# Seven block products in place of eight for the second half's in-projection of a hybrid decoder trunk

## The chip, the cores and the metric

The kernel runs on one core of a Trainium2 chip. The metric is the device time of one execution in microseconds (us), lower is better. PE is the matrix engine, DVE the vector engine, ACT the scalar engine, POOL and SP the engines that in this kernel mostly issue DMAs.

## The reference

One layer of a decoder trunk over 2048 positions of 1024 channels (D_MODEL), one batch. A first projection gives 3584 channels: 1024 each for the recurrent unit's input and its gate, 512 each for the short convolution's b, c and x.

```python
h = rms_norm(x, norm1_g)
z = h @ w_in                                   # 1024 -> 3584
lru_x, lru_gate, sc_b, sc_c, sc_x = split(z)
lru_x = causal_dwconv(lru_x, lru_conv_w) + lru_conv_b      # 4 taps
r = sigmoid(lru_x @ wa + ba); i = sigmoid(lru_x @ wx + bx) # 64x64 per head
a = exp(-8 r softplus(-lam)); h_t = a_t h_{t-1} + sqrt(1 - a_t^2) i_t lru_x_t
y_mix = [h * gelu(lru_gate), sc_b * causal_dwconv(sc_c * sc_x, sc_conv_w)]
x = x + y_mix @ w_out                          # 1536 -> 1024
u = causal_dwconv(rms_norm(x, norm2_g) @ w_up, ffn_conv_w) # 1024 -> 6144, 3 taps
gate, up = split(u)
x = x + (gelu(gate) * up) @ w_down             # 3072 -> 1024
return rms_norm(x, final_g)
```

## The kernel before

Channels lie on the partitions and positions on the free axis; x comes transposed. The positions are done in two halves of 1024 (T), and a half in two blocks of 512 (NB). Every product of two float32 numbers is made of three matmuls of rounded parts: `split(hi, lo, src)` copies the operand to its rounded high part on ACT and subtracts that from it on DVE for the low part; then hi x hi, hi x lo and lo x hi are summed in PSUM.

The program's stages in order: the in-projection and mixers of half 0 (`in_phase(0, ...)`), the out-projection of half 0 (`sweeps(0, ..., "o", ...)`, "output sweep 0"), the same two for half 1, then for each half an up phase (`up_phase`) and a down sweep.

`in_phase` walks over 12 units (`UNITS`): 8 units L (a 128-channel piece of the recurrent unit: input, convolution, gates, scan) and 4 units S (short convolution). For each product it loads a 512 KB column of w_in (`load_weights`, `load_parts`), splits it and runs 8 contraction steps x 3 matmuls x 2 blocks of 128x512 = 48 matmuls (`product_step`, L238). 28 products make a half. `lru_gates` (L320) runs the gate matmuls of 64 rows, `lru_scan` the sigmoids, exp, root and the scan. The results y of pairs of units are combined (`combine_even`, `combine_odd`) into sums for the out-projection and stored to DRAM (`y_d`); such stores wait in a list (`defer`) and are issued a few steps later by `tick`.

Out-projection, up and down already work by blocks: a 2x2 block product takes seven products of sums for eight. The sums of the weights, S1 to S4, are made by accumulating DMAs (`sum_step`, w_out's during half 0, w_down's during half 1, a piece is loaded to DRAM through SP, and the addition is issued on POOL) or, in the up phase, by DVE (`up_weights`). The up phase's products are `Pair`s: the terms W11, S1, S2, S3, W22, S4, W12 of 12 matmuls each (L613), whose running sums are copied from PSUM by ACT (L624) and added by DVE (L628). `h_prep` makes the right operands for it: x2 times gain and 1/rms, the differences and sums of its blocks, split. In output sweep 0 x of half 1 is prepared (`x_prep`) and its squares are summed; the sweeps also sum the squares of x2 (`add_squares`).

A sweep goes through seven groups of three steps; each step loads 512 KB of weights and 512 KB of y (`wrw_o`, `wrf_o`), splits both (`wh_o`, `wl_o`, `fh_o`, `fl_o`) and runs 24 matmuls (L733).

The order on PE, SP and POOL is as the program is written; that on ACT and DVE is set by a scheduler with priorities (`high_priority`, the constants HP, HW and so on). Buffers are pages of 128x1024 in tagged pools: "act" 28, "w" 10 for split weights, "tmp" 7, and raw tiles `wr`, 4 of three blocks each. A tile waits until the page that it takes is free.

Of the kernel before, what the change touches and what calls it, by code (L numbers as in the profile page):

```python
# [12 lines left out]
P = 128  # L13
# [9 lines left out]
UNITS = [(u[0], int(u[1])) for u in "L0 L1 S0 L2 L3 S1 L4 L5 L6 L7 S2 S3".split()]  # L23
EPS = 1e-6
HP = 120
HALVES = (slice(0, P // 2), slice(P // 2, P))
# [27 lines left out]
PLACE = {"11": (0, 0), "12": (0, 1), "21": (1, 0), "22": (1, 1)}  # L54

# [14 lines left out]
def block_kernel(  # L70
# [43 lines left out]
    sd_d = blocks("sd_d", S_OPS, NI)  # L114
    x2_d = [[dr.tile([2, P, T], F32, name=f"x2_d{h}_{m}") for m in range(KC // 2)] for h in range(NH)]
# [10 lines left out]

    def wpage(name):
        return page(name, "w", 10)
# [7 lines left out]
    def raw_tile(name):  # L136
        return sb.tile([P, 3, NB], F32, name=name, tag="wr", bufs=4)
# [7 lines left out]
    def flat(t):  # L145
        return t.rearrange("p a b -> p (a b)")
# [34 lines left out]
    waiting = []  # L181
    pieces = []
# [3 lines left out]
    def defer(n, dst, src):  # L186
        waiting.append([n, dst, src])

    def tick():
        for w in waiting:  # L190
            w[0] -= 1
        due = [w for w in waiting if w[0] <= 0]
        waiting[:] = [w for w in waiting if w[0] > 0]
        for _, dst, src in due:
            nc.sync.dma_start(dst, src)
# [9 lines left out]

    gate_w = []

    def load_gates():
        gate_w.append(flat(tmp("gw")).rearrange("p (c k) -> p c k", c=NLRU))
        nc.sync.dma_start(gate_w[0], w_gate.rearrange("c p k -> p c k"))  # L210
# [14 lines left out]
    def load_weights(src, name):  # L225
        out = next(load_parts(src, name, 1))
        tick()
        return out

# [73 lines left out]
    def lru_conv(c, half, ps, rs):  # L303
# [3 lines left out]
        cv = flat(act(f"cv{half}_{c}"))  # L307
# [8 lines left out]
    def lru_gates(c, half, cv):  # L316
        pss = [pst2(f"z{name}{half}_{c}") for name in "ri"]
        for t in range(T // NB):
            for ps, rows in zip(pss, HALVES):
                nc.tensor.matmul(ps[t], gate_w[0][rows, c, :], cv[rows, blk(t)], start=True, stop=True)  # L320
        return pss

    def lru_scan(c, half, cv, g, *gates):
        n = f"{half}_{c}"
        r, i, a = (flat(act(f"{x}{n}")) for x in "ria")
# [20 lines left out]
        nc.scalar.activation(g, g, AF.Gelu_apprx_tanh)  # L346
        nc.vector.tensor_tensor(h, g, h, ALU.mult)
        return h
# [9 lines left out]
    def in_product(o, half, acts):  # L358
        ps = pst2(f"zin{half}_{o}")
        wts = load_weights(w_in[o], f"in{half}_{o}")  # L360
# [10 lines left out]
    def sc_first(s, half, acts, rs, ps):  # L371
# [3 lines left out]
        pr = with_halo(f"pr{half}_{s}", 2, half, p_halo[:, s, :], 1, nc.vector)  # L375
# [36 lines left out]
    def in_phase(half, acts, acc, between):  # L412
        if half == 0:
            acts = []
            raws = [raw_tile(f"wr_{half}_{i}") for i in range(3)]
            firsts = (0, NLRU, 1)
            loads = [
                load_parts(w_in[o], f"in{half}_{o}", KC // 2, tile_=t) for o, t in zip(firsts, raws)
            ]
            wts = [None, None, None]  # L420
            pss = [pst2(f"zin{half}_{o}") for o in firsts]
            xs = []
            for k in range(KC):
                def first_part():
                    wts[0] = next(loads[0])

                hi, lo, x = x_prep(half, k, 2 if k < 2 else 1, None if k else first_part)
                acts.append((hi, lo))
                xs.append(x)
                for i in range(1, 3) if k == 0 else range(2 if k in (1, 3, 5) else 0):  # L430
                    wts[i] = next(loads[i])
                for ps, wt in zip(pss[: 3 if k < 2 else 2], wts):
                    product_step(ps, wcol(wt, k), acts[k], k == 0, k == KC - 1)
                if k == 2:
                    nc.sync.dma_start(prm, par[:, KC:])
            for k in range(KC):
                x_square(half, k, acc, xs[k])
            for _ in loads[2]:
                pass
            load_gates()  # L440
        else:
            pss = [in_product(o, half, acts) for o in (0, NLRU)]
        parts = mean_split(acc, f"a{half}")
        rss = []

        def mean():
            rss.append(inv_rms(acc, f"a{half}", parts))
            nc.gpsimd.tensor_copy(mark, rss[0][:, 0:1])
            ready.append(True)

        if half == 0:
            mean()
            ps_2 = pss[2]
            for k in range(2, KC):
                product_step(ps_2, wcol(wts[2], k), acts[k], False, k == KC - 1)
            sum_step()
        else:
            ps_2 = None
            mean()
        rs = rss[0]  # L460
        cv = lru_conv(0, half, pss[0], rs)
        if half == 0:
            decay_rates(dz)
        cur = (cv, lru_gate(0, half, pss[1], rs))
        ps_n = None
        for n, (kind, c) in enumerate(UNITS):
            nxt = UNITS[n + 1] if n + 1 < len(UNITS) else None
            if kind == "L":
# [6 lines left out]
                gates = lru_gates(c, half, cv)  # L475
# [5 lines left out]
            else:  # L481
                pr = sc_first(c, half, acts, rs, ps_n)
                y = sc_second(c, half, acts, rs, pr)
# [4 lines left out]
            last = n >= NOUT - 2  # L488
            if n % 2 == 0:
                even, yc = y, flat(tmp(f"yc{half}_{n}"))  # L490
                combine_even(y_d[half], 4 if last else 7, n // 2, even, yc)
            else:
# [546 lines left out]
```

## Time and profile before

| | |
|---|---|
| median of 3 runs | 2273.15 us (2273.06 to 2275.95) |
| profiled execution | 2274.76 us |
| its span | 2273.0 us |
| granted clock of PE | 0.998 |
| busy time of PE, DVE, ACT, POOL | 2256.1, 1703.8, 1161.1, 138.0 us |
| in-projection of half 0 and output sweep 0 | 0 to 330, 330 to 444 us |
| in-projection of half 1 and output sweep 1 | 444 to 767, 767 to 884 us |
| up, down of half 0 | 884 to 1341, 1341 to 1570 us |
| up, down of half 1 | 1570 to 2029, 2029 to 2273 us |

The span runs from the first to the last instruction in the trace of one execution; the execution's own time is a little longer. A row of groups gives an engine's line and operation, the tile written and those read, shapes, a count, and after the bar the busy time, the mean of one in ns, and the idle time before them with what ended it. A row of the chain gives start, duration and the number of instructions run through.

### The profile page before, as it was taken

The numbers are of one execution on the slowest core, as the hardware profiler recorded it, in microseconds if no ns is written. First come the engines' busy times: TensorE is split into PE (matmuls) and PEld (weight loads), VectorE is DVE, ScalarE is ACT, GpSimd is POOL, SyncE is SP. The second block draws the span as 40 slices with busy tenths as digits, with TensorE's granted clock in tenths as the row PEclk, the third lists the DMA queues.
The fourth block names the chain that finished last, engine by engine and source line by source line (L and its number), as shares of the span: only waits on it lengthen the run. The fifth ranks groups of instructions, "written<-read, shape, count | busy, mean of one in ns | idle before, by whom it ended". The sixth has DMA issues, their size and how long they took to land.

```text
span 2273.0 us, 26022 instructions
## 1 busy us (share of the span) xinstructions
PE 2256.1 (99%) x9918; PEld 1847.4 (81%) x9918; DVE 1703.8 (75%) x1924; ACT 1161.1 (51%) x1279; POOL 138.0 (6%) x188
## 2 busy tenths in 40 slices
PE   9999999999999999999999999999999999999997
PEld 7877788878877888888888888888888888888886
DVE  8765668757657798888888887586888888876556
ACT  7564825565576355544444444354544444443343
POOL 0100000011000000111111100000100000000000
PEclk9999999999999999999999999999999999999999
DMA  8732238768754585233333357675233232359755
GB/s 280 189 95 76 105 129 297 273 163 216 208 116 148 177 284 201 97 110 100 105 104 102 107 197 257 212 252 193 70 102 116 89 118 91 116 183 322 259 195 176
DMA packets 145180, 376.69 MB, mean 166 GB/s; under 512 B 13920, under 2 KB 16608, under 8 KB 144480
## 3 DMA queue, kind: packets, MB, share of 16 engines
q1 hardware_dynamic: 135120, 356.17, 45.2%
q0 software_dynamic: 9792, 18.88, 5.2%
q8 instruction: 77, 1.26, 0.2%
q14 instruction: 47, 0.39, 0.1%
q10 hardware_dynamic: 144, 0.00, 0.0%
HBM read 287.96 MB, written 124.78 MB: 182 GB/s over the span
## 4 chain that ended last, share of the span: by engine, by line
PE 97%; DVE 1%; DMA 1%; issue 0%; ACT 0%; DVEq 0%
PE zin_b L238 27%; PE zx L613 23%; PE zc L613 11%; PE dx L733 11%; PE dy L733 9%; PE za L613 6%; PE ox L733 6%; PE oy L733 4%; PE zr_b L320 1%; DMA wrb_up<-in_w_up 0%; DVE x2r L914 0%; DMA g<-in_par 0%; DVE x2r L770 0%; DVE fl_d L199 0%; DVE fl_o L199 0%
## 5 line engine op out<-in xcount | busy, mean ns | idle before, releaser
L238 PE MATMUL zin_b<-xh,wh_in 128*128 128x512 f32 x896 | 278.1, 391 | 0.9 <-ACT wh_in L198 0.8
L238 PE MATMUL zin_b<-xl,wh_in 128*128 128x512 f32 x896 | 276.2, 389 | 0.1
L238 PE MATMUL zin_b<-xh,wl_in 128*128 128x512 f32 x896 | 275.9, 389 | 0.0
L238 PEld LDWEIGHTS zin_b<-xh,wh_in 128*128 128x128 f32 x896 | 167.0, 188 | 47.2 <-issue 6.8
L238 PEld LDWEIGHTS zin_b<-xl,wh_in 128*128 128x128 f32 x896 | 168.2, 188 | 35.6 <-DVE xl L402 0.6
L238 PEld LDWEIGHTS zin_b<-xh,wl_in 128*128 128x128 f32 x896 | 168.2, 188 | 35.0
L199 DVE TENSOR_TENSOR fl_d<-wrf_d,fh_d 128x1024 fp32r<-128x1024 f32 x84 | 102.8, 1224 | 123.6 <-ACT fh_d L198 121.1
L198 ACT ACTIVATE fh_d<-wrf_d 128x1024 fp32r<-128x1024 f32 x84 | 89.0, 1060 | 205.1 <-PE dy L733 85.1
L199 DVE TENSOR_TENSOR wla_up<-wra_up,wha_up 128x1024 fp32r<-128x1024 f32 x48 | 58.8, 1226 | 141.3 <-ACT wha_up L198 141.3
L733 PE MATMUL dx<-fh_d,wh_d 128*128 128x512 f32 x384 | 149.4, 389 | 0.0
L733 PE MATMUL dx<-fl_d,wh_d 128*128 128x512 f32 x384 | 149.4, 389 | 0.0
L733 PE MATMUL dx<-fh_d,wl_d 128*128 128x512 f32 x384 | 149.4, 389 | 0.0
L198 ACT ACTIVATE wh_in<-wr_in 128x1024 fp32r<-128x1024 f32 x53 | 55.6, 1054 | 169.7 <-PE zin_b L238 127.8
L613 PE MATMUL zc<-hhB,whd_up 128*128 128x512 f32 x384 | 126.0, 389 | 0.0
L299 DVE SCALAR_TENSOR_TENSOR cu<-un,prm,cu 128x1024 f32<-128x1024 f32 x96 | 122.7, 1278 | 4.3 <-ACT cu L295 4.3
L299 DVE SCALAR_TENSOR_TENSOR cg<-ug,prm,cg 128x1024 f32<-128x1024 f32 x96 | 123.0, 1282 | 0.4
L624 ACT ACTIVATE ug<-zx 128x512 f32<-128x512 f32 x96 | 57.6, 600 | 126.0 <-PE zx L613 126.0
L613 PE MATMUL zx<-ht,whc_up 128*128 128x512 f32 x384 | 118.2, 389 | 0.0
L733 PE MATMUL dy<-fh_d,wh_d 128*128 128x512 f32 x288 | 112.0, 389 | 0.0
L733 PE MATMUL dy<-fl_d,wh_d 128*128 128x512 f32 x288 | 112.0, 389 | 0.0
L733 PE MATMUL dy<-fh_d,wl_d 128*128 128x512 f32 x288 | 112.0, 389 | 0.0
L199 DVE TENSOR_TENSOR wl_d<-wrw_d,wh_d 128x1024 fp32r<-128x1024 f32 x84 | 102.4, 1220 | 11.6 <-ACT wh_d L198 10.3
(257 smaller groups left out, 5531.5 us busy)
## 6 DMA issues: line engine op xcount, KB each, us to landing
wr_in<-in_w_in SPq DMA_DIRECT2D x53, 512.0 KB, 7.0
wra_up<-in_w_up SPq DMA_DIRECT2D x48, 512.0 KB, 4.5
wrb_up<-in_w_up SPq DMA_DIRECT2D x48, 512.0 KB, 5.2
f_d_T<-cg SPq DMA_DIRECT2D x96, 256.0 KB, 2.5
wrw_d<-sd_d_S SPq DMA_DIRECT2D x48, 512.0 KB, 4.6
wrf_d<-f_d_T SPq DMA_DIRECT2D x48, 512.0 KB, 3.7
f_d_B<-cu SPq DMA_DIRECT2D x72, 256.0 KB, 2.4
wrw_d<-in_w_down SPq DMA_DIRECT2D x36, 512.0 KB, 4.6
```

Source lines behind the costliest of these rows:

```text
L198: nc.scalar.activation(r32(hi), src, AF.Copy)
L199: nc.vector.tensor_tensor(r32(lo), src, hi, ALU.subtract)
L238: nc.tensor.matmul(ps[t], r32(a), r32(b[:, blk(t)]), start=(first and i == 0), stop=(last and i == 2))
L299: nc.vector.scalar_tensor_tensor(dst, src[:, k : k + T], col(o_w + k), dst, ALU.mult, ALU.add)
L320: nc.tensor.matmul(ps[t], gate_w[0][rows, c, :], cv[rows, blk(t)], start=True, stop=True)
L613: nc.tensor.matmul(ps, r32(p[:, s]), r32(self.hs[k][x][o]), start=f and i == 0, stop=l and i == 2, skip_group_check=True,)
L624: nc.scalar.activation(dst, self.x, AF.Copy)
L733: nc.tensor.matmul(ps[m], r32(p), r32(x[:, k, :]), start=first and i == 0 and n == 0, stop=(last or not on_x) and i == ni - 1 and n == 2, ...
```

## The change

The in-projection of half 1 is made by `in_blocks` with `InPair`s. Two of the 28 products make a pair (`PAIRS`, `BLOCKS`): the input and the gate of a unit L, c and x of a short convolution, b of two short convolutions. A pair is a 2x2 block product (two columns of weights, two blocks of positions, contraction over 2 x 512) by seven terms of 12 matmuls. Its weight sums S1 to S4 are made in the first half by DVE (`pair_sums`, while the raw columns are there) and stored to DRAM, `si_d`, 28 stores of 512 KB. The right operands are made in output sweep 0 (`x1_prep`, four sets) in place of the eight `x_prep`. The squares of half 1's x are summed in the first half from x read once more; those of x2 beside the blocks and the up phase, from x2 read back (`squares_then_mean`).

The terms of neighbouring pairs are interleaved on PE: step j runs W11 and W12 of pair j, W22 of pair j-1, the open gates, S2 of j, S4 of j-1, S1 and S3 of j. The first pair of the blocks and of each up phase is spread: all seven terms of one contraction step, then of the next, in seven PSUM banks. The units' order becomes L0 L1 S0 S1 L2 to L7 S2 S3. A store of y or si_d in the two in-projections is issued on POOL (`store_queue`), without delay in the blocks. Raw tiles become 6 of two blocks. The "w" pages are divided in 2 "w" and 8 "v"; block weights are loaded through the 2 (`in_weights`). The first three steps of output sweep 1 take their split pages from "act" with a higher priority (`LEAD`, `LW`).

```diff
@@
+PAIRS = [(u[0], int(u[1])) for u in "L0 B0 L1 X0 L2 X1 L3 L4 L5 B2 L6 X2 L7 X3".split()]
+TERMS = [("W11", "B11"), ("S1", "T1"), ("S2", "T2"), ("S3", "T3"), ("W22", "T4"), ("S4", "B22"), ("W12", "B21")]
+NW = 2
+NWV = 10
+NR = 6
+LW = 400
+LEAD = 3
@@
     def wpage(name):
-        return page(name, "w", 10)
+        turn[0] += 1
+        return wv_page(name, "w" if turn[0] * NW % NWV < NW else "v")
@@
     def raw_tile(name):
-        return sb.tile([P, 3, NB], F32, name=name, tag="wr", bufs=4)
+        return page(name, "wr", NR)
@@
     def defer(n, dst, src):
-        waiting.append([n, dst, src])
+        if n == 0:
+            store_queue[0].dma_start(dst, src)
+        else:
+            waiting.append([n, dst, src])
...
         for _, dst, src in due:
-            nc.sync.dma_start(dst, src)
+            store_queue[0].dma_start(dst, src)
@@
+    def pair_sums(a, b):
+        if a not in raw_of or b not in raw_of:
+            return
+        i, _ = PAIR_OF[a]
+        ra, rb = raw_of.pop(a), raw_of.pop(b)
+        sa, sb_ = act(f"sa{i}"), act(f"sb{i}")
+        with tc.high_priority(offset=HW):
+            for t, x, y in (
+                (sa[:, 1, :], rb[:, 0, :], rb[:, 1, :]),
...
+            ):
+                nc.vector.tensor_tensor(t, x, y, ALU.add)
+        defer(0, si_d[i][:, 0:2, :], sa)
+        defer(0, si_d[i][:, 2:4, :], sb_)
@@
+    def in_weights(ops):
+        n = "_".join(f"{i}{op}" for i, op in ops)
+        raw, m = wv_page(f"wr_in{n}", "w"), len(ops)
+        for at, (i, op) in enumerate(ops):
+            if op in KEPT:
+                o, h = BLOCKS[PAIRS[i]][op[1] == "2"], slice(0, NB) if op[2] == "1" else slice(NB, T)
+                src = w_in[o][:, h]
+            else:
+                src = si_d[i][:, SPILLED.index(op), :]
+            nc.sync.dma_start(raw[:, at, :], src)
...
+            split(t[:, 0, :], t[:, 1, :], raw[:, at, :])
@@
+        for j in range(count + 1):
+            tick()
+            load(*uses(j + 1), rest=j + 1 >= count)
...
+            if cur:
+                cur.first_term()
+                cur.second_term()
+            if prev:
+                prev.seventh_term()
+            for name in open_gates:
+                gated, scanned = gates.pop(name)
+                scanned(gated())
+            open_gates = []
+            if cur:
+                cur.fourth_term()
+            if prev:
+                prev.sixth_term()
+                finish(prev)
+            open_gates = list(gates)
+            if cur:
+                cur.third_term()
+                cur.fifth_term()
@@
-                with tc.high_priority(offset=HW):
+                with tc.high_priority(offset=LW if step < lead else HW):
                     for raw, n in zip(raws, "wf"):
-                        home = act if tail and last and i2 >= ni // 2 - 2 else wpage
+                        home = act if step < lead or tail and last and i2 >= ni // 2 - 2 else wpage
@@
-        if s % 2 == 0 and 2 <= s <= 2 * KC:
-            hi, lo, x = x_prep(1, len(x1))
-            x_square(1, len(x1), ss1[1], x)
-            x1.append((hi, lo))
+        if s in (2, 6, 11, 16):
+            hx.append(x1_prep(len(hx), ss1[1]))
@@
-    in_phase(
-        1,
-        x1,
-        ss1[1],
-        beside_mixers,
-    )
+    store_queue[0] = nc.gpsimd
+    late_gates = in_blocks(hx, beside_blocks)
+    store_queue[0] = nc.sync
```

In the up phase the weights now come in three loads a pair (W11, W12, and W22 with W21) instead of two.

How the instructions move, at three places. First SP at the end of output sweep 0. Before, the last load of the sweep (`wrf_o0_6_2`) is followed by the first columns of w_in for half 1 and stores of x2 (`x2_d0`); the words in brackets are what an instruction waits for:

```order
L746 DMA wrf_o0_6_2_3390<-y_d0_T4_2_107 128x1024 [waits DMAHW5_49,DVE_49]
L220 DMA wr_in1_0_3438<-in_w_in 128x1024 [waits DMAHW6_49,DMAHW0_49,DVE_49]
L195 DMA x2_d0_0_249<-xr0_12_0_2690 128x2x512 [waits DMAHW7_49,DVE_49]
L195 DMA x2_d0_1_250<-xr0_12_1_2737 128x2x512 [waits DVE_49]
L220 DMA wr_in1_8_3496<-in_w_in 128x1024 [waits DMAHW1_49,DVE_49]
L195 DMA x2_d0_2_251<-xr0_21_0_3360 128x2x512 [waits DMAHW2_49,DVE_49]
```

After, the loads of single blocks of weights (`wr_in0W11_0S1` is the page for W11 and S1 of pair 0) follow, from w_in and from the stored sums `si_d`:

```order
L1005 DMA wrf_o0_6_2_3579<-y_d0_T4_2_107 128x1024 [waits DMAHW0_49,DVE_49]
L816 DMA wr_in0W11_0S1_3618<-in_w_in 128x512 [waits DMAHW1_49,DVE_49,PE_49]
L816 DMA wr_in0W11_0S1_3618<-si_d0_249 128x512 [waits DMAHW2_49]
L816 DMA wr_in0S2_0S3_3627<-si_d0_249 128x512 [waits DMAHW3_49,DVE_49,PE_49]
L816 DMA wr_in0S2_0S3_3627<-si_d0_249 128x512 [waits DMAHW4_49]
L816 DMA wr_in0W22_0S4_3636<-in_w_in 128x512 [waits DMAHW2_49,DMAHW5_49,DMAHW1_49,DVE_49]
L816 DMA wr_in0W22_0S4_3636<-si_d0_249 128x512 [waits DMAHW6_49]
L816 DMA wr_in0W12_1W11_3647<-in_w_in 128x512 [waits DMAHW4_49,DMAHW7_49,DMAHW3_49,DVE_49]
L816 DMA wr_in0W12_1W11_3647<-in_w_in 128x512 [waits DMAHW0_49]
```

The first loads wait on PE now, and a load of 512 KB has become two of 256 KB. The stores of x2 stand ahead of them.

Second DVE at the start of output sweep 1. `fl_o1_1_0` is the low part of y for the sweep's fourth step, `wl_o` that of weights; `sv`, `yc` and `yd` belong to the last short convolution, `xr1` are the sweep's first sums, from PSUM `ox1`. Before:

```order
L510 SCALAR_TENSOR_TENSOR yc1_10_5411<-yc1_10_5411,sv1_3_5567 128x512
L199 TENSOR_TENSOR wl_o1_0_2_5667<-wrw_o1_0_2_5662,wh_o1_0_2_5666 128x1024
L511 SCALAR_TENSOR_TENSOR yd1_11_5572<-yc1_10_5411,sv1_3_5567 128x512
L199 TENSOR_TENSOR fl_o1_0_2_5671<-wrf_o1_0_2_5664,fh_o1_0_2_5670 128x1024
L199 TENSOR_TENSOR wl_o1_1_0_5713<-wrw_o1_1_0_5708,wh_o1_1_0_5712 128x1024
L199 TENSOR_TENSOR fl_o1_1_0_5717<-wrf_o1_1_0_5710,fh_o1_1_0_5716 128x1024
L770 TENSOR_TENSOR xr1_11_0_5636<-xr1_11_0_5636,ox1_0_5577 128x512
L770 TENSOR_TENSOR xr1_11_0_5636<-xr1_11_0_5636,ox1_1_5578 128x512
L770 TENSOR_TENSOR xr1_11_1_5674<-xr1_11_1_5674,ox1_2_5579 128x512
```

After, with `i1_7`, `r1_7` (gates and scan of unit L7), `soin12` (gate of L7), `yc1_8` (combination for y):

```order
L390 TENSOR_TENSOR i1_7_5833<-i1_7_5833,cv1_7_5778 128x1024
L558 SCALAR_TENSOR_TENSOR yc1_10_5666<-yc1_10_5666,soin9_5189 128x512
L393 SCALAR_TENSOR_TENSOR r1_7_5832<-a1_7_5834,h_last_84,i1_7_5833 128x1024
L1029 TENSOR_TENSOR xr1_11_1_5978<-xr1_11_1_5978,ox1_2_5890 128x512
L398 TENSOR_TENSOR soin12_5695<-soin12_5695,r1_7_5832 128x1024
L1029 TENSOR_TENSOR xr1_11_0_5940<-xr1_11_0_5940,ox1_1_5889 128x512
L556 TENSOR_TENSOR soin10_5365<-soin12_5695,soin10_5365 128x512
L557 SCALAR_TENSOR_TENSOR yc1_8_5630<-yc1_8_5630,soin12_5695 128x512
L229 TENSOR_TENSOR fl_o1_1_0_6021<-wrf_o1_1_0_6014,fh_o1_1_0_6020 128x1024
L558 SCALAR_TENSOR_TENSOR yc1_8_5630<-yc1_8_5630,soin12_5695 128x512
```

The split of the fourth step's y (`fl_o1_1_0`) stood ahead of the sweep's first sums (`xr1`); it now stands behind L7's scan (L393) and two of these sums.

Third POOL at the end of the blocks. Before, its last rows ahead of the up phase are additions of w_down's sums:

```order
L356 DMA sd_d_S4_1_244<-sd_d_S2_1_232 256x512 [waits DMAHW0_49,DMASW7_49,DMASW1_49]
L356 DMA sd_d_S4_2_245<-sd_d_S2_2_233 256x512 [waits DMAHW2_49,DMASW2_49]
L356 DMA sd_d_S4_3_246<-sd_d_S2_3_234 256x512 [waits DMAHW6_49,DMASW3_49]
L356 DMA sd_d_S4_4_247<-sd_d_S2_4_235 256x512 [waits DMAHW0_49,DMASW4_49]
L356 DMA sd_d_S4_5_248<-sd_d_S2_5_236 256x512 [waits DMAHW7_49,DMASW5_49]
```

After, ten stores of y end the blocks (`soin10`, `soin12`, `yc1_8`, `yc1_10`, `soin9` and `sbin9` are the pages that hold y and its combinations):

```order
L215 DMA y_d1_T2_2_122<-yc1_8_5630 128x512 [waits DMASW1_49,DVE_49]
L215 DMA y_d1_B21_2_113<-soin12_5695 128x512 [waits DMASW2_49,Activation_49]
L215 DMA y_d1_T3_2_125<-soin10_5365 128x512 [waits DMASW3_49]
L215 DMA y_d1_B22_2_116<-soin12_5695 128x512 [waits DMASW4_49]
L215 DMA y_d1_T4_2_128<-yc1_8_5630 128x512 [waits DMASW5_49,DVE_49]
L215 DMA y_d1_T2_2_122<-yc1_10_5666 128x512 [waits DMASW6_49]
L215 DMA y_d1_B21_2_113<-soin9_5189 128x512 [waits DMASW7_49]
L215 DMA y_d1_T3_2_125<-sbin9_5058 128x512 [waits DMASW0_49]
L215 DMA y_d1_B22_2_116<-soin9_5189 128x512 [waits DMASW1_49]
L215 DMA y_d1_T4_2_128<-yc1_10_5666 128x512 [waits DMASW2_49]
```

The stores stood on SP before.

510 lines of the change are left out of this document (364 added, 146 removed).

## The prediction

> **What bounds the kernel now.** I read the page first, then the waits of PE, the chain of work, and the busy time by stage.
>
> ```profile
> span 2273.0 us, 26022 instructions
> PE 2256.1 (99%) x9918; PEld 1847.4 (81%) x9918; DVE 1703.8 (75%) x1924; ACT 1161.1 (51%) x1279; POOL 138.0 (6%) x188
> PE 97%; DVE 1%; DMA 1%; issue 0%; ACT 0%; DVEq 0%
> ```
> ```profile
> PE oy L733 <- DVE fl_o L199: 1.5, 2, 0.9
> PE zx L613 <- ACT ug L624: 1.2, 1, 1.2
> ```
> PE is the bound from end to end: 2256.1 of 2273.0 us busy, 97% of the chain, and its largest wait on another engine is 1.5 us. So a matmul that is taken away shortens the kernel by its full price, as long as the operands still come in time, and every new stall is added in full.
>
> What one matmul costs must be read from the chain, since matmuls overlap:
>
> ```profile
> 329.60 16.32 PE ox L733 x72
> 443.84 21.76 PE zin_b L238 x96
> 488.27 0.62 PE zr_b L320
> 488.90 0.42 PE zr_b L320
> 1341.63 32.64 PE dx L733 x144
> ```
> ```profile
> L238 PE MATMUL zin_b<-xh,wh_in 128*128 128x512 f32 x896 | 278.1, 391 | 0.9 <-ACT wh_in L198 0.8
> ```
> 16.32/72, 21.76/96 and 32.64/144 all give 0.2267 us from one matmul to the next. The 391 ns of the group's row are one matmul's duration, much of it under its neighbours. A unit's gate matmuls take 0.62 + 3 x 0.42 = 1.9 us.
>
> ```profile
> 0.00:330.00 330.00, 327.98 (x1433) 262.13 (x1434) 216.57 (x276) 198.83 (x216) 12.36 (x19) 1.00 0.48 148
> 330.00:444.00 114.00, 114.00 (x505) 94.42 (x504) 97.01 (x109) 62.51 (x63) 0.00 (x0) 1.00 0.73 256
> 444.00:767.00 323.00, 323.00 (x1415) 258.24 (x1414) 207.93 (x215) 184.54 (x192) 21.62 (x25) 1.00 0.63 178
> 768.00:884.00 116.00, 114.52 (x504) 94.17 (x503) 105.75 (x120) 56.63 (x59) 0.33 (x4) 1.00 0.72 250
> 884.00:1341.00 457.00, 457.00 (x2017) 378.40 (x2017) 375.71 (x434) 229.15 (x273) 62.67 (x91) 1.00 0.32 109
> ```
> The columns are the window and its length, the busy time of PE, PEld, DVE, ACT and POOL, the granted clock, the DMA engines' share and GB/s. The windows are the first half's in-projection, output sweep 0, the second half's in-projection, output sweep 1, the first up phase. In the in-projections DVE and ACT are busy two thirds of the time or less; in both sweeps DVE is at 85 to 91%, so what reaches a sweep late has little slack to catch up in.
>
> The prices of the small work, from the groups by form (from 440 to 770 us, and of the up phase for the last row) and the DMA rows:
>
> ```profile
> L330 ACT ACTIVATE r<-zr_b,prm 64x512 f32<-64x512 f32 x16 | 11.0, 685 | 0.3
> L330 ACT ACT_TABLE_LOAD x8 | 10.3, 1283 | 0.1
> L297 ACT ACTIVATE cv<-xl,prm 128x1024 f32<-128x1024 f32 x8 | 9.9, 1244 | 8.2 <-DVE xl L369 8.2
> L335 ACT ACTIVATE a<-r,nc 128x1024 f32<-128x1024 f32 x8 | 9.2, 1153 | 0.1
> L339 ACT ACTIVATE cv<-cv 128x1024 f32<-128x1024 f32 x8 | 8.5, 1063 | 0.1
> L199 DVE TENSOR_TENSOR wl_in<-wr_in,wh_in 128x1024 fp32r<-128x1024 f32 x27 | 32.9, 1219 | 17.6 <-ACT wh_in L198 17.6
> L299 DVE SCALAR_TENSOR_TENSOR cv<-xl,prm,cv 128x1024 f32<-128x1024 f32 x24 | 30.8, 1284 | 1.5 <-ACT cv L297 0.9
> L343 DVE TENSOR_TENSOR_SCAN r<-a,h_last,i 128x1024 f32<-128x1024 f32 x8 | 18.8, 2350 | 0.2
> L369 DVE TENSOR_TENSOR xl<-zin_b,ss_a 128x512 f32<-128x512 f32 x16 | 10.3, 685 | 18.8 <-PE zin_b L238 18.7
> ...
> L624 ACT ACTIVATE ug<-zx 128x512 f32<-128x512 f32 x48 | 28.8, 600 | 64.4 <-PE zx L613 64.4
> ```
> ```profile
> wr_in<-in_w_in SPq DMA_DIRECT2D x53, 512.0 KB, 7.0
> ...
> y_d_T<-yc SPq DMA_DIRECT2D x24, 256.0 KB, 2.4
> ...
> sd_d_S<-in_w_down POOLq DMA_DIRECT2D x12, 512.0 KB, 5.7
> ...
> x<-in_xT SPq DMA_DIRECT2D x4, 256.0 KB, 4.2
> ```
> ```profile
> 472.93 0.89 POOL L356 DMA_DIRECT2D sd_d_S<-in_w_down  x1 [0.42 <-issue]
> 478.65 0.90 POOL L356 DMA_DIRECT2D sd_d_S<-in_w_down  x1 [4.83 <-issue]
> 484.61 0.89 POOL L356 DMA_DIRECT2D sd_d_S<-in_w_down  x1 [5.06 <-issue]
> ```
> The last fence is POOL's timeline: it issues an accumulating DMA every 5.7 to 6.0 us, busy 0.9 us for each, and the idle rest is charged to nothing but "issue". That is the landing time of the row above (5.7): one such DMA is under way at a time.
>
> **The saving.** The group's three like forms hold 3 x 896 = 2688 matmuls for both halves, 1344 for the second. Seven terms for eight make 14 pairs x 7 x 12 = 1176. 168 matmuls x 0.2267 us = **38.1 us** off. A term is 12 x 0.2267 = 2.72 us, a pair 19.04, with gates 20.9. The floor is a span of 2234.9.
>
> **First half, added: nothing, range 0 to 7.** 56 additions of 128x512 are 38.6 us on DVE (0.69 each), the squares moved here 8 of 1.22 and 8 of 1.06 on ACT: DVE 216.6 + 38.6 + 9.8 = 265 of 330. It hides behind PE as long as DVE keeps some of the 65 us left. The DMA engines take 14.7 MB of sums and 4.2 MB of x more, on 148 GB/s x 330 us = 49 MB at a share of 0.48: about 0.66. POOL gets 28 sum stores and 37 y stores beside 12 accumulations. Price of a POOL store, which no row shows: at least its issue, 0.9 us; at most a landing and an issue with one under way at a time, 2.4 + 0.9, about 3.4. I take 1.3, nearer to the lower end, because an accumulation also reads what it adds to, and nothing in the program waits between plain stores. At 1.3 POOL is busy 12 x 5.8 + 65 x 1.3 = 154 of some 297 us; at 3.4 it is 291, and the last y of the first half reach output sweep 0 some 7 us late.
>
> **Output sweep 0, changed: nothing.** Eight preparations of x (1.28, 1.22 and 1.22 on DVE, 29.8 in all) and eight additions of squares (9.8) leave; four operand sets come (2 x 1.28 + 5 x 0.69 + 3 x 1.22 = 9.7 each, 38.7). The sum stays at 96 of 114, beside PE; each us that DVE is late there would show on PE only past the 18 left. x2's squares, read back from DRAM, go to the blocks and the up phase: eight passes of 1.06 on ACT and eight additions of 1.22 each, in the slack of DVE (115 of 323, 81 of 457).
>
> **Start of the blocks: +6, range 2 to 10.** The two pages that the first weights go through still hold sweep 0's last operands, one until 5.4 us before its end (a step of 24 matmuls), one until its end; SP waits there, with all later weights and the pieces of w_down's sums queued behind it. Seven terms need four fillings of these two pages, and the spread first pair wants all seven within its first k. Filling three is issued when filling one is split, about 2 us after the sweep's end, and filling four after filling two (landing 4.2, two splits of 0.6 + 0.69): about 6.5. It lands about 3 later, and W12's split is done at 10. The pair's other three k-rounds (3 x 4.76 us) follow: 24.9 instead of 19.0. With 2.4 for a landing it is 2; with the 7.0 of the loads before, 10.
>
> **Steps 8 to 10 of the blocks: +5, range 2 to 8.** Pairs L3, L4 and L5 follow each other. Between the third copy of pair 7 and the second of pair 10, ACT's order has 22 splits and 11 copies of 128x512 (33 x 0.6 = 19.8), 24 sigmoids (16.4), 8 table loads (10.3) and 14 passes of 128x1024 (1.06 to 1.24, 15.6): 62.1 us. PE needs two pairs with gates, four terms and gates in this time: 41.8 + 12.7 = 54.5. ACT is 7.6 late; the next use of that bank comes 5.4 later, which leaves 2.2 if the cover is whole, all 7.6 if the weights' splits behind are wanted first. I take the middle.
>
> **Start of output sweep 1: +10, range 6 to 27.** Before, DVE had the first split of sweep step 3 (`fl_o1_1_0`) done ahead. Now unit L7 ends in the sweep. Its gates end 2.7 us before the sweep starts (one term follows), and the first sigmoid's table load comes 1.9 before that. On ACT come, from the first sigmoid to the square root, 8 sigmoids (5.5), 3 splits (3.2), three table loads (3.8), exp, three more passes and the root (5.6), 18.1 us: until 13.5 into the sweep. On DVE follow the product, an addition, the scan of 2.35, five more rows (among them two sums of sweep results), then `fl_o1_1_0`: 9.5 us, so 23. PE wants it after step 2, 3 x 5.44 = 16.3: 6.7 late. Next, `fl_o1_1_1` stands 9.1 us (ten rows) behind it, and PE wants it 5.44 later: 3.7 more. Queued behind are the `ha`, `hb` sets of the up phase, early enough. The upper end is the POOL price again: the pages that the next splits need are freed by the last y stores, ten of them in a row on POOL; at 3.4 each the splits come 27 late, at 1.3 not later than DVE's own.
>
> **Elsewhere: +1** for the spread first pair and the third load in the up phases (DVE is busy 376 of 457 us there).
>
> Sum: 2273.0 - 38.1 + 6 + 5 + 10 + 1 = 2256.9. The profiled execution took 2274.76, 1.8 more than its span and 1.6 more than the median of the runs (2273.15), so the forecast is **2257 us**, 0.7% below.
>
> The Trainium skill ("DMA: Bandwidth & Descriptors", "Issuing engines are not separate DMA queues") says that DMAs from any engine run on the same 16 DMA engines, and that another issuing engine saves only issue time. This speaks against any gain from the stores' move to POOL; the trace of before issues them on SP alone and cannot show it. The same page ("Anatomy of one DMA") gives an estimate of 2.0 us plus 0.6 for 256 KB on this path: one at a time, 2.6 a store; by it the sum would be some 10 us higher.
>
> **Rivals.**
> The covers hold (0.25): all stalls small, span 2235 to 2243, so 2240. For it: the averages of DVE and ACT. Against it: the three orders above.
> POOL's stores go one at a time (0.13): 27 instead of 10 at sweep 1, 7 at sweep 0: 2257 + 24 = 2281, slower. For it: the 5.7 us rhythm above. Against: a plain store reads less. It decides from about 3 us a store, where the blocks' 24 x 5.8 + 42 x 3 = 265 of 281 us leave nothing.
> Stores as slow as accumulations (0.04): the first half needs 12 x 5.8 + 65 x 5.8 = 447 us of POOL in 297; 2273 - 38 + 150, about 2385.
> The matmul's price is 0.39 (0.02): 168 x 0.39 = 66, 2208; the chain's rows speak against it.
>
> The likeliest case (0.56) runs from 2246 to 2268. With the covers holding and the milder end of the stores' rival, the range is 2238 to 2275; it leaves out the lowest end of the covers' case (0.06) and the upper ends (0.13). A change within 0.2% (2268.6 to 2277.7) is about what cannot be told from none. Of the likeliest case 0.02 and of the stores' rival 0.05 lie within it. Faster: 0.25 + 0.54 + 0.02 = 0.81; within: 0.02 + 0.05 = 0.07; slower: 0.08 + 0.04 = 0.12.
>
> **What the new profile would show.** PE with 168 matmuls fewer, and three idle stretches: after sweep 0's end on the splits of S2, W12 or on a load, inside the blocks on ACT's copies, at the new sweep 1's third step on `fl_o1_1_0` (L229). POOL's issues of y stores closer than 2 us. Wrong would be the forecast if PE waits there on stores (waits naming POOL's queue at the sweeps), or if the up phases grow over 457 us.

## The result and the profile after

The changed kernel takes 2309.57 us (median of 4 runs, 2307.49 to 2310.52) against 2273.36 us for the kernel before, run beside it: a ratio of 1.0154, 95% interval 1.0141 to 1.0167. It is slower by 36 us; the forecast was 2257, the range 2238 to 2275.

The page after:

```profile
span 2308.7 us, 26404 instructions
PE 2242.5 (97%) x9750; PEld 1825.3 (79%) x9750; DVE 1787.3 (77%) x2070; ACT 1214.7 (53%) x1403; POOL 179.0 (8%) x298
PE 65%; issue 2%; ACT 2%; DVE 2%; DMA 1%; POOL 0%; SPq 0%; DVEq 0%; ACTq 0%; POOLq 0%
```

PE runs 9750 matmuls for 9918, the 168 fewer of the prediction. But its share of the chain falls from 97 to 65%, and its busy time falls by only 13.6 us where 168 matmuls are 38.1. The waits of PE, the longest first in total, and the windows of the four stages that changed (columns as in the prediction):

```profile
PE oy L992 <- DVE fl_o L229: 10.7, 4, 5.9
PE zr_b L369 <- DVE cv L345: 6.9, 3, 4.4
PE zxin L666 <- ACT xlin L677: 5.6, 2, 3.7
PE zxin L666 <- ACT soin L677: 5.6, 3, 4.6
PE zxin L666 <- DVE wW_in L229: 5.5, 2, 3.5
```
```profile
0.00:336.70 336.70, 330.80 (x1435) 263.45 (x1436) 261.76 (x344) 210.77 (x228) 48.31 (x84) 0.99 0.61 194
336.70:457.60 120.90, 115.41 (x505) 94.23 (x504) 104.56 (x119) 52.84 (x56) 1.45 (x2) 1.00 0.71 257
457.60:789.50 331.90, 300.78 (x1245) 232.11 (x1245) 213.15 (x263) 225.90 (x300) 40.29 (x57) 0.96 0.72 202
789.50:920.50 131.00, 119.85 (x506) 97.64 (x505) 120.33 (x133) 66.84 (x71) 6.52 (x13) 0.95 0.77 272
```

The granted clock stands third from the end of a row. The table puts this together; "half clock" is the length of the stage times what the clock lacks to 1.

| stage | before, us | after, us | PE idle after | half clock after |
|---|---|---|---|---|
| in-projection, half 0 | 329.4 | 336.7 | 5.9 | 1.7 |
| output sweep 0 | 114.2 | 121.0 | 5.5 | 0 |
| in-projection, half 1 (the blocks) | 323.6 | 331.9 | 31.1 | 13.7 |
| output sweep 1 | 116.4 | 130.9 | 11.2 | 6.8 |
| up 0, down 0, up 1, down 1 | 1389.5 | 1388.4 | 12.5 | 4.8 |

Over the whole span PE is idle 66.2 us where it was 16.8. The half clock comes to 27.0 us where it was 4.4; but of these 4.8 and 4.4 lie behind PE's last matmul and cost nothing, so 22.2 are new. So -38.1 + 49.4 + 22.2 = 33.5 of the 35.7 us between the spans. The blocks should take 323.6 - 38.1 = 285.5; they take 46 more, and this stage alone turns the gain into a loss.

The half clock was in no term of the prediction. Three windows around the first half's longest wait show it: PE idles 2.6 us up to 104.67 us, and the 4 us that follow run at 0.57.

```profile
96.00:104.00 8.00, 6.06 (x27) 4.69 (x25) 8.00 (x10) 2.97 (x3) 0.00 (x0) 1.00 1.09 357
104.00:108.00 4.00, 3.33 (x8) 2.68 (x9) 4.00 (x7) 1.45 (x2) 1.47 (x2) 0.57 1.08 430
108.00:116.00 8.00, 8.00 (x37) 6.59 (x36) 7.77 (x10) 2.80 (x3) 0.74 (x2) 1.00 0.98 302
```

The Trainium skill ("TensorE: Matmul & The Clock Gate", "What's actually happening") states that PE falls to half clock after an idle window of about 3.4 us and needs a busy one to come back. The trace agrees that the clock is either whole or half (0.50 in the last window shown here); but here a gap of 2.6 us was enough, while output sweep 0, whose longest gaps are 2.3 and 2.0 us (the waits of PE in that window), kept 1.00. No limit can be read from the length of one gap either: at the start of the blocks two waits of 0.6 and 1.1 us, at 459 and 460 us, were followed by the window below.

```profile
PE oy L992 <- DVE fl_o L229: 2.8, 2, 2.3
PE ox L992 <- DVE fl_o L229: 2.7, 2, 2.0
```
```profile
462.80:469.40 6.60, 4.71 (x10) 2.85 (x10) 2.59 (x4) 2.41 (x4) 0.00 (x0) 0.50 0.61 215
```

### The profile page after: what moved, and what is told of

It is laid out like the page before. It is cut to its first block, busy times and chain, and to the rows that moved or that the text cites. A ratio compares the mean times of both kernels' runs of the same rounds, so it can differ in the third digit from the quotient of the medians.

```text
span 2308.7 us, 26404 instructions
## 1 busy us (share of the span) xinstructions
PE 2242.5 (97%) x9750; PEld 1825.3 (79%) x9750; DVE 1787.3 (77%) x2070; ACT 1214.7 (53%) x1403; POOL 179.0 (8%) x298
## 4 chain that ended last, share of the span: by engine, by line
PE 65%; issue 2%; ACT 2%; DVE 2%; DMA 1%; POOL 0%; SPq 0%; DVEq 0%; ACTq 0%; POOLq 0%
PE zx L666 22%; PE dx L992 11%; PE zc L666 11%; PE dy L992 8%; PE za L666 5%; PE ox L992 2%; PE oy L992 2%; PE zxin L666 1%; PE zS L666 1%; PE zW L666 1%; PE zcin L666 0%; DMA sx_b<-x_d 0%; DMA wr_in9S_9S<-si_d 0%; DMA sd_d_S<-in_w_down 0%; ACT r L380 0%
## 5 line engine op out<-in xcount | busy, mean ns | idle before, releaser
L284 PE MATMUL zin_b<-xh,wl_in 128*128 128x512 f32 x448 | 138.7, 391 | 2.6 <-DVE wl_in L229 2.6
L284 PE MATMUL zin_b<-xh,wh_in 128*128 128x512 f32 x448 | 139.7, 393 | 0.7 <-ACT xh L452 0.4
L284 PE MATMUL zin_b<-xl,wh_in 128*128 128x512 f32 x448 | 138.7, 390 | 0.1
L666 PE MATMUL zc<-hhB,whd_up 128*128 128x512 f32 x368 | 120.8, 389 | 0.0
L666 PE MATMUL zx<-ht,whc_up 128*128 128x512 f32 x368 | 113.3, 389 | 0.0
L284 PEld LDWEIGHTS zin_b<-xh,wh_in 128*128 128x128 f32 x448 | 83.7, 188 | 24.4 <-DVE yc L557 1.5
L284 PEld LDWEIGHTS zin_b<-xh,wl_in 128*128 128x128 f32 x448 | 84.5, 189 | 20.6 <-DVE wl_in L229 3.0
L228 ACT ACTIVATE fh_o<-wrf_o 128x1024 fp32r<-128x1024 f32 x42 | 44.5, 1059 | 106.5 <-PE ox L992 28.3
L284 PEld LDWEIGHTS zin_b<-xl,wh_in 128*128 128x128 f32 x448 | 84.4, 188 | 18.1 <-DVE xl L453 0.5
```

The costliest lines, as they stand in the source:

```text
L228: nc.scalar.activation(r32(hi), src, AF.Copy)
L284: nc.tensor.matmul(ps[t], r32(a), r32(b[:, blk(t)]), start=(first and i == 0), stop=(last and i == 2))
L666: nc.tensor.matmul(ps, r32(p[:, s]), r32(self.hs[k][x][o]), start=f and i == 0, stop=l and i == 2, skip_group_check=True,)
```

## The experiments

Every kernel below is the changed one with the edit shown. Stage times are from its profile. Where an edit leaves work out, its expectation says which.

**Output sweep 1.** PE's two longest waits there are at the step that the prediction named, the sweep's fourth: first for the high part of y from ACT, then for `fl_o1_1_0`, as predicted. Rows of PE's timeline, then of DVE's:

```profile
808.83 0.51 PE L992 MATMUL oy<-fh_o,wh_o 128*128 128x512 f32 x1 [2.82 <-ACT fh_o L228]
815.26 0.80 PE L992 MATMUL oy<-fl_o,wh_o 128*128 128x512 f32 x1 [5.92 <-DVE fl_o L229]
```
```profile
808.21 2.34 DVE L393 TENSOR_TENSOR_SCAN r<-a,h_last,i 128x1024 f32<-128x1024 f32 x1
...
813.99 1.22 DVE L229 TENSOR_TENSOR fl_o<-wrf_o,fh_o 128x1024 fp32r<-128x1024 f32 x1
```

`fl_o1_1_0` stands behind the scan and ends 25.7 us into the sweep (23 forecast). The first edit moves it ahead:

```diff
-LEAD = 3
+LEAD = 4
```

> LEAD 4 for 3: the fourth step of output sweep 1 takes its split pages from the act pool and its splits get the high priority too. Theory (the place of fl_o1_1_0 in DVE's order, behind L7's scan, makes sweep 1's stall): the idle 11.2 us at the sweep's start and the 6.8 us that PE runs at half clock there mostly go, 2309.6 - 18 = 2292, range 2288 to 2300. Rival (the pages are freed late by the last y stores): the wait only moves to the next split, under 5 us gained, 2305 to 2310.

Measured 2310.46 us (ratio 1.0159, 1.0144 to 1.0174): nothing gained. In this kernel's chain the fifth step now waits for a page that a store of L7's y holds:

```profile
815.33 0.24 DMA y_d_T<-soin
815.57 1.15 DVE fl_o L229
816.72 0.04 issue
816.76 7.20 PE oy L992 x19
```

So the rival holds: the place in DVE's order was not alone; both it and the pages end with L7, some 24 us into the sweep. In the changed kernel too the chain stands 6.5 us on the landing of a store of L7's y (`y_d_T<-soin`, from 815.6 us). The second edit leaves the wait and fills it:

```diff
+                if half == 1 and name == "o" and step == 3:
+                    for _ in range(24):
+                        nc.tensor.matmul(ps[0][:, :P], ones, ones, start=True, stop=True, skip_group_check=True)
```

> 24 idle matmuls of ones (128x128) put on PE where it waits for the fourth step of output sweep 1; nothing else changed. Theory (idle PE is followed by stretches of half clock, which cost beside the idle time): the clock stays at 1.00 in that sweep, 5 to 7 us gained, 2303. Rival (the low clock has another cause, or the stalls alone make the loss): no gain, 2309 to 2312.

Measured 2307.71 us (1.0148, 1.0133 to 1.0163). The sweep went from 130.9 to 126.5 us. The same two windows, of the changed kernel and then of the filled one:

```profile
806.00:816.00 10.00, 1.26 (x4) 0.83 (x4) 10.00 (x12) 1.06 (x1) 1.57 (x3) 0.74 0.61 222
816.00:826.00 10.00, 8.03 (x24) 5.77 (x22) 7.27 (x9) 2.85 (x3) 3.84 (x8) 0.74 0.97 338
```
```profile
806.00:816.00 10.00, 6.71 (x53) 6.26 (x52) 10.00 (x12) 1.06 (x1) 1.71 (x4) 0.93 0.63 227
816.00:826.00 10.00, 8.63 (x32) 6.41 (x32) 8.49 (x10) 3.91 (x4) 3.69 (x7) 0.90 0.99 345
```

The clock is 0.93 and 0.90 for 0.74 twice. The half clock's cost in the sweep falls from 6.8 to 1.7 us: idling does cost beside the idle time, and useless matmuls give some of it back. In the whole kernel's time the gain (1.9 us) is within the intervals; only the stage shows it, and up phase 0 takes 1.5 of it back (459.4 us for 457.8).

To test L7 itself, its convolution, gates and scan were left out:

```diff
+            if pair.kind == "L" and pair.unit == 7:
+                nc.scalar.activation(pair.other, pair.other, AF.Gelu_apprx_tanh, scale=-1.0)
+                nc.vector.tensor_tensor(pair.other, pair.other, pair.first[:, 3 : 3 + T], ALU.mult)
+                keep_y(half, n, pair.other, (0, 0))
```

> Unit L7 of the second half leaves out its convolution, gates and scan; its y is gelu of the gate times its input. Theory (L7's end, 24 us into output sweep 1, holds the pages and DVE's turn): the 11 us of idle and 7 of half clock in sweep 1 go, PE has 1.9 less of gates: 2309.6 - 20 = 2290, range 2285 to 2295. Rival (the sweep's start is late without L7 too: loads, stores, the operand sets): 2298 to 2307.

Measured 2300.35 us (1.0112, 1.0095 to 1.0128); the sweep 121.3 us, idle 4.3 and half clock 1.7. The whole time lies in the rival's range, not in the theory's: L7 makes 9.6 of the 14.5 us that the sweep grew, and 4.9 stay. What holds those is not settled; the chain of this kernel stands on the landing of another y store there:

```profile
801.40 10.17 DMA y_d_T<-sbin
```

**POOL's stores.** The first three of seven y stores in a row on POOL:

```profile
581.90 0.59 POOL L215 DMA_DIRECT2D y_d_T<-yc  x1 [22.05 <-DVE yc L557]
582.48 0.57 POOL L215 DMA_DIRECT2D y_d_B<-soin  x1
583.04 0.54 POOL L215 DMA_DIRECT2D y_d_T<-soin  x1
```

A store takes 0.54 us, and the next goes at once. The prediction's range for it, 0.9 to 3.4, was too high. One edit tests the move to POOL as a whole:

```diff
-    store_queue = [nc.gpsimd]
+    store_queue = [nc.sync]
...
-    store_queue[0] = nc.gpsimd
+    store_queue[0] = nc.sync
```

> All stores issued by SP as in the kernel before, none on POOL. The prediction's rival (POOL's store queue is what costs): 2275 to 2290. Theory now (a store on POOL takes 0.54 us and nothing waits for POOL but the last pages of sweep 1): within 3 us of 2309.6, or slower by 5 to 30, because SP's loads then stand behind stores that wait for their data.

Measured 2439.49 us (1.0735, 1.0715 to 1.0755): 130 us slower. The waits of SP and of PE in it:

```profile
SPq L215 <- DVE sa L272: 271.3, 14, 32.7
SPq L215 <- DVE yc L557: 84.6, 4, 33.2
```
```profile
PE zin_b L284 <- ACT wh_in L228: 50.4, 12, 13.8
PE ox L992 <- ACT fh_o L228: 38.3, 2, 32.9
```

On SP a store that waits for its data holds up every load behind it. The first half grows from 337 to 413 us, the blocks from 332 to 401. The sentence of the Trainium skill ("DMA: Bandwidth & Descriptors", "Issuing engines are not separate DMA queues") that the prediction drew on, that another issuing engine saves only issue time, leaves this out: here the place behind a waiting instruction is worth 130 us. It is the price of this change's stores, many of them issued without delay: the kernel before stored from SP too, SP stood up to 43.0 us at one of them (`SPq L195 <- DVE r L347`), and PE did not wait for it.

**The blocks: pages, order and loads.** First, more pages for the loads:

```diff
-NW = 2
+NW = 4
```

> NW 4 for 2: four pages for the block weights on their way in, six for the rest. Theory (the blocks' stalls come from loads that wait for one of two pages and then land 4 to 8 us later): the blocks' idle time of 31 us falls by 10 to 20 and the half clock with it, 2285 to 2300. Rival (ACT and DVE in their fixed order are what is late): 2306 to 2312.

Measured 2332.61 us (1.026, 1.0243 to 1.0277). PE now waits 39.9 us for ACT's copies `soin`, whose "v" pages are 6 in place of 8. Its waits for the weights' splits in the blocks fall from 12 us to 3, but it comes late to them, so this only shows that the "v" pages are tight too; it gives no price for the loads.

Next, all later loads left out, by splitting two kept pages again and again:

```diff
-        raw, m = wv_page(f"wr_in{n}", "w"), len(ops)
+        m = len(ops)
+        if len(kept_raw) == 2:
+            raw = kept_raw[took[0] % 2]
+            took[0] += 1
...
```

> The blocks load weights twice only (four block loads); every later weight is split again from these two pages, so the sums of the second half are made of wrong weights, and all the other work is the same. Theory L (loads through two pages, landing 4 to 8 us, make the blocks' stalls): the blocks' idle time falls from 31 to 12 us or less and the half clock's loss from 14 to 5, 2309.6 - 27 = 2283, range 2275 to 2292. Rival A (ACT and DVE run their fixed order late): at most 6 us gained, 2303 to 2310.

Measured 2278.05 us (1.0014, 1.0005 to 1.0024), the blocks 299.3 us with 9.9 idle and 3.4 of half clock. ACT and DVE do all that they did before, in the same stage: theory L is right, the loads (their waits for pages and their landing together) make 33 of the 46 us. But these loads are 25.7 MB and land in 2.6 to 11.7 us (median 4.4); what makes some of them late? SP's timeline in the changed kernel:

```profile
641.26 0.80 SPq L816 DMA_DIRECT2D wr_in7S_8S<-si_d  x2
642.12 2.06 SPq L1140 DMA_DIRECT2D sx_b<-x_d  x1
644.22 1.13 SPq L404 DMA_DIRECT2D sd_d_S<-in_w_down  x2
645.46 0.92 SPq L816 DMA_DIRECT2D wr_in8S_9W<-si_d  x1
646.42 0.52 SPq L816 DMA_DIRECT2D wr_in8S_9W<-in_w_in  x1
648.34 0.81 SPq L816 DMA_DIRECT2D wr_in9W_8W<-in_w_in  x2
662.24 0.80 SPq L816 DMA_DIRECT2D wr_in9S_8S<-si_d  x2
```

One row of the waits of SP in the blocks shows how long a load waits for its page (total, times, longest):

```profile
SPq L816 <- DVE wW_in L229: 103.3, 17, 15.3
```

SP waits for a page, up to 15 us, and then issues in one burst two blocks of weights, a 512 KB load of x2 for its squares, two pieces of 512 KB for the sums of w_down, and four more blocks. These four, which a next step needs, stand behind 1.5 MB. Three edits take parts of this out. Without seven of x2's loads and squares, without the squares alone, without the loads alone:

```diff
-            if 0 <= k < KC:
+            if 0 <= k < (1 if name == "b0" else KC):
...
-            if 1 <= k <= KC:
+            if 1 <= k <= (1 if name == "b0" else KC):
```
```diff
-            if 1 <= k <= KC:
+            if 1 <= k <= (1 if name == "b0" else KC):
```
```diff
+            if name == "b0" and 0 < k < KC:
+                held.append(held[0])
...
```

> Seven of the eight loads, squares and additions of half 0's x2 beside the blocks are left out (the mean is then of one part). Theory Q (ACT stands behind a square that waits for its load, 4.9 us in all, and so the copies behind it come late): 5 to 10 us gained, 2300 to 2305. Rivals L and A: 8 us less on ACT of 236, 0 to 4 us gained, 2305 to 2310.

> The eight loads of half 0's x2 beside the blocks stay, seven of the eight squares and additions are left out (the mean is then of one part). Theory W (what costs is ACT standing at a square whose load is late, and the 7.4 us of squares on it): as without the loads too, 2288, range 2285 to 2292. Rival S (the loads take SP's and the DMA engines' time from the weights): 2300 to 2309.

> The eight squares and additions beside the blocks stay, but all read the first load; seven loads are left out (the mean is then of one part taken eight times). Theory W, the wait part: squares that never wait give back half or more of the 22 us, 2290 to 2299. If the work on ACT and DVE alone is what costs: 2300 to 2309.

Measured: 2287.80 us (1.0064, 1.0049 to 1.0079) without both, 2305.27 (1.0133, 1.0116 to 1.0150) with the loads alone, 2293.97 (1.0084, 1.0069 to 1.0099) with the squares alone. The blocks took 310.8, 327.2 and 313.7 us. So seven loads of 512 KB cost 16 us of 22, and 17 where nobody waits for them (2305.27 to 2287.80); the work on ACT and DVE costs 4 to 6. The last number lies in theory W's range too, but the loads alone, at 2305, do not: W falls, S stands. Then the sums, out of the blocks into up phase 0:

```diff
     def beside_blocks(j):
         mean0(j)
-        sum_step()
-        sum_step()
...
+    def beside_up(j):
+        mean1(j)
+        sum_step()
+        if j < 4:
+            sum_step()
...
```

> All 24 sums of w_down are made beside up phase 0 in place of the blocks; nothing else changes. Theory S (SP issues the blocks' weights, x2's loads and two 512 KB pieces of the sums in one burst, and the weights land behind them): the blocks go from 332 to about 312 and the up phase stays at 458: 2309.6 - 20 = 2290, range 2284 to 2300. Rival (x2's loads were the whole of it): 2303 to 2310. If POOL's copies in the up phase wait behind the accumulations and PE with them: above 2310.

Measured 2287.97 us (1.0058, 1.0043 to 1.0073), 21.6 less than with the change alone. The blocks' window and the landings of three loads of weights, in this kernel, and the same loads in the changed one:

```profile
457.70:763.70 306.00, 291.69 (x1245) 227.52 (x1244) 213.17 (x263) 225.16 (x300) 18.68 (x34) 0.98 0.43 142
```
```profile
wr_in2W_2W<-in_w_in SPq DMA_DIRECT2D x2, 256.0 KB, 2.7
wr_in4W_4W<-in_w_in SPq DMA_DIRECT2D x2, 256.0 KB, 3.3
wr_in5W_4W<-in_w_in SPq DMA_DIRECT2D x2, 256.0 KB, 2.8
```
```profile
wr_in2W_2W<-in_w_in SPq DMA_DIRECT2D x2, 256.0 KB, 5.8
wr_in4W_4W<-in_w_in SPq DMA_DIRECT2D x2, 256.0 KB, 5.8
wr_in5W_4W<-in_w_in SPq DMA_DIRECT2D x2, 256.0 KB, 8.7
```

ACT and DVE are as busy as before (225 and 213 us), the DMA engines at 0.43 for 0.72, these three loads land in a third to 0.57 of the time (over all of the stage's weight loads the median falls from 4.4 to 3.2 us), and 26 us of the blocks' 46 are gone. Theory S is confirmed as to the price. The up phase bears the sums without a loss (457.9 us).

What delays the weights is not settled between the order in SP's queue and the load on the DMA engines, and the edit also takes POOL's additions out of the stage. The stage's mean share does not decide it: without x2's loads it stays at 0.73 (both with the squares alone and with the squares in the sweep, below), and yet the blocks are 18 to 22 us shorter. While the burst shown above lands, the engines of the changed kernel are nearly full (share of the DMA engines, second from the end of a row):

```profile
641.00:648.00 7.00, 7.00 (x27) 5.61 (x26) 4.30 (x7) 1.86 (x3) 0.90 (x1) 0.81 0.89 221
648.00:656.00 8.00, 8.00 (x36) 5.46 (x35) 1.54 (x2) 6.42 (x8) 0.90 (x1) 1.00 0.98 295
```

With the sums begun in the first half instead:

```diff
     sums(w_out, so_d, NO)
+    sums(w_down, sd_d, NI)
...
```

> The sums of w_down begin in the first half, as soon as w_out's are through, and go on beside the blocks with one piece a step in place of two. Theory D (the DMA engines' load in the blocks makes the weights land late): 3 to 8 us gained, 2302 to 2306. Rivals: none in the blocks, and 0 to 5 us lost in the first half, 2308 to 2315.

Measured 2316.06 us (1.0182, 1.0165 to 1.0199): the blocks 323.6 at a share of 0.56, but output sweep 0 grew from 121.0 to 135.2. Where the sums go matters: up phase 0 took them with its share rising from 0.36 to 0.60, while the first half and sweep 0 stood at 0.61 and 0.71 without them. That the share is the reason is not shown. The squares of x2, put back into output sweep 0 as before the change, alone and with the sums late:

```diff
+    ss2[0] = acc_tile("b0")
...
-        store_done(x2_d[0], None, "b0"),
+        store_done(x2_d[0], ss2[0], "b0"),
...
+    mean0 = late_mean(ss2[0], "b0", rs2[0], 1)
```

> The squares of half 0's x2 are summed in output sweep 0 from the pages there, as in the kernel before; no loads and squares of it beside the blocks. Theories W and S alike: the blocks lose 20 us, output sweep 0 gains up to 6 (ten us more on DVE, busy 102 of 121 there): 2290, range 2286 to 2297. If the pages or DVE in the sweep are too tight: 2300 or more.

> The sums of w_down beside up phase 0 and the squares of x2 back in output sweep 0: the blocks' loads are weights alone. Theory S: the blocks come to 300, near the 299 without the later weight loads, sweep 0 is 9 longer than with the squares away: 2309.6 - 32 + 9 = 2287, range 2278 to 2294. If the two shares do not add (each only frees the other's place): 2290 to 2299.

Measured 2298.60 us (1.0103, 1.0088 to 1.0118) and 2292.78 (1.0080, 1.0065 to 1.0095). The blocks took 310.3 and 306.6, the sweep 129.7 and 128.9. With the sums late the blocks take 306 with x2's loads and without: the two gains do not add. The squares cost the sweep 8 to 9 us. A lower priority for the operands did not help it:

```diff
-LP = 0
+LP = 200
```

> As the kernel with late sums and squares in the sweep, and LP 200: the operand sets (x1_prep, h_prep) take a lower priority on ACT and DVE than the sweeps' splits. Theory (sweep 0's idle comes from the operands' instructions ahead of the splits of y on DVE): sweep 0 back from 130 to about 117, others as they were: 12 less than the kernel without LP, about 2275, range 2268 to 2285. Rival (DVE has too much to do there in any order, and the blocks then start later): 0 to 4 less, 2283 to 2290.

Measured 2292.54 us (1.0077, 1.0062 to 1.0092), above both ranges, and sweep 0 129.6: the lower place of the operands does not help. That DVE, busy 112 us of the sweep, has too much to do there in any order is likely and not shown.

**The order of the pairs.** Never three units L in a row, with L7 one pair earlier; the same with the squares back and LEAD 5; with the sums late; and another order with the wait filled:

```diff
-PAIRS = [(u[0], int(u[1])) for u in "L0 B0 L1 X0 L2 X1 L3 L4 L5 B2 L6 X2 L7 X3".split()]
+PAIRS = [(u[0], int(u[1])) for u in "L0 B0 L1 X0 L2 L3 X1 L4 L5 B2 L6 L7 X2 X3".split()]
```

> PAIRS as L0 B0 L1 X0 L2 L3 X1 L4 L5 B2 L6 L7 X2 X3: never three units L in a row, and L7 one pair earlier, so that its y is done some 19 us before output sweep 1. Theory A (ACT is overloaded by L3 L4 L5, and L7 ends late in the sweep): sweep 1's 11 us of idle and 7 of half clock go and the blocks gain 0 to 8, 2309.6 - 20 = 2290, range 2283 to 2300. Rival L (loads): the blocks keep their idle time, only part of sweep 1's goes, 2298 to 2310.

> The squares back in output sweep 0, PAIRS with never three units L in a row and L7 one pair earlier, and LEAD 5. If the page waits of sweep 1 come from L7's late end: 2290 less the 11 us of idle and 7 of half clock there, and 0 to 4 back in the blocks, 2276, range 2270 to 2285. If order and LEAD only move the wait, as with LEAD 4 alone: 2288 to 2296.

> The late sums and PAIRS as L0 B0 L1 X0 L2 L3 X1 L4 L5 B2 L6 L7 X2 X3. Theory A: the blocks 306 to 299, and sweep 1 133 to 124, since L7 ends a pair earlier: 2272, range 2266 to 2282, and so no slower than the kernel before. Rival (as with the sums in the blocks: the order brings nothing): blocks 306 to 312, sweep 128 to 133, 2283 to 2293.

> The late sums, PAIRS as L0 L1 B0 L2 X0 L3 X1 L4 B2 L5 L6 X2 L7 X3 (two units L in a row at most, L7 where it was), and 24 idle matmuls in sweep 1's wait. Theory A for the rest of the blocks' idle (ACT overloaded by L3 L4 L5): 306 to 299 or less with the half clock, sweep 1 133 to 128 by the clock: 2276, range 2270 to 2284. Rival (the idle only moves to other units L): blocks 304 to 312, 2282 to 2290.

Measured 2313.75 us (1.0173, 1.0158 to 1.0189), 2310.18 (1.0153, 1.0138 to 1.0168), 2297.17 (1.0095, 1.0078 to 1.0112) and 2289.62 (1.0068, 1.0053 to 1.0083). No order is better than the change's own, and the first three are slower than even their rivals' ranges; with the sums late, the blocks took 320.1 and 313.5 us for 306.0. The idle time moves to other units L: in the first of these two, PE waits 5.7, 3.9 and 4.4 us at the gates of L3, L4 and L7. No version tried beats the kernel before.

## Why the prediction was wrong, point by point

The saving was right: 168 matmuls. What failed is the cover.

- **The step that failed is the cover of the blocks: their loads had no term.** The prediction costed SP's queue only at the start of the blocks and put nothing down for the weights' loads through two pages after that, nor for x2's reads. The blocks' 46 us too many fall by 33 without the later weights' loads, by 26 with the sums out, and by 18 without seven of x2's loads; these shares overlap. The sums stood beside this stage before too (share 0.63 there, 0.72 now) and PE did not wait; beside the new loads they cost. The step that put x2's squares "in the slack of DVE" looked at the wrong engine: their loads alone cost 16.
- **The half clock was missing.** About 22 us beyond the idle time; it makes each us of idle cost about 1.4 in the changed stages. No row of the kernel before could have shown its size: PE's longest wait there is 1.2 us, and its half clock lies behind PE's last matmul.
- **Start of the blocks, 6:** 3.65 us of idle and 3.4 of half clock, 7. The place is right (waits on the splits of S1, S2, W22 and S4); that the sum is too is luck, as the half clock makes up for idle time that did not come.
- **L3, L4, L5, 5:** in the changed kernel PE waits there 4.6 us for a copy of ACT, as predicted (but ACT had just stood 3.0 us for a load of weights), and 1.7 and 4.4 us at the gates of L4 and L5, for the convolution on DVE (`cv`). With the sums late the copy's wait is gone and 5.7 and 1.7 us at these gates remain. So the place is right, the engine only in part; and since other orders only moved the waits, "three L in a row" alone is not the cause.
- **Output sweep 1, 10:** 11.2 of idle, at the step named; `fl_o1_1_0` came within 3 us of the time named. The sweep grew by 14.5, since the half clock comes on top. The cause is wider than DVE's order: the pages wait for L7's y too.
- **Elsewhere, 1:** the four later stages took 1.1 less; a wait of 1.2 us in the second up phase is gone. Of the wrong sign, and small.
- **First half and output sweep 0, nothing:** 7.3 and 6.8. DVE's sum for the sweep was 96 us and measured 104.6. The term that was mis-sized is what leaves the sweep: the prediction counts three DVE rows for a preparation of x, 29.8 us for the eight, and the kernel before has one, 10.2 us (the row below). With both groups of squares (8.5 and 6.9) 25.6 us leave in place of 39.6; the four operand sets come to 38.5, as forecast. Nor does the slack of 18 us cover it: PE waits 5.5 us for `fl_o` from DVE. The first half's longest wait, 2.6 us, is on a low part of the weights from DVE. What sets the rest of the first half was not tried.

```profile
L402 DVE SCALAR_TENSOR_TENSOR xl<-x,g,xh 128x1024 fp32r<-128x1024 f32 x8 | 10.2, 1281 | 0.7 <-ACT xh L401 0.7
```

- **The stores' rival** came nearer to the time (2281) than the forecast, still 28 us off, and for the wrong reason: a store takes POOL 0.54 us, and they do not go one at a time. What it had right is that the last y stores hold pages at output sweep 1; there it is the late y and the landing of 6.5 us that count.

## What to carry to other kernels

When PE is never idle, the saving is easy and the cover is everything: list, queue by queue, what is issued in the same burst as the data that PE waits for next, and count that as delay; judge the DMA engines by their share during the burst, not by the mean of the stage. Put work that nobody needs soon into a stage with idle DMA engines: here moving the sums was worth 22 us. Count what leaves a stage from the rows of the kernel before, as carefully as what comes. And where PE will idle, add the half clock to the idle time: here some 0.4 us for each us of it.

## What the runs showed that was not expected

A store issued on POOL takes 0.54 us of it, with the next one at once, while accumulating DMAs come at least 5.7 us apart; the change's stores on SP cost 130 us. A gap of 2.6 us was enough for 3.4 us at half clock, and at the start of the blocks two waits of 0.6 and 1.1 us close together stood ahead of such a stretch. And seven loads of 512 KB cost 16 us, most of it without anyone waiting for their data.
